# Depthwise taps of the last two tiles, layer norm and second pointwise product taken chunk by chunk, without products on diagonals

## The chip, the core and the metric

The kernel runs on one core of a Trainium2 chip. The metric is the device time of one execution in microseconds (us), the median over several runs. The engines of the core run in parallel: PE (TensorE, matrix products), DVE (VectorE, elementwise), ACT (ScalarE, elementwise with functions and scales), POOL (GpSimd, elementwise) and the queues that issue transfers (SP). Each engine works through its own list of instructions in order, and waits at an instruction until what it needs has been signalled by the others.

## The reference

One step of a two-layer diffusion backbone over 1152 tokens (1024 of a sample, 128 of a prompt) of 1024 features. Layer 0 mixes tokens with a gated depthwise convolution, layer 1 with attention; each is followed by a feed-forward part. Only layer 0's mixer changes here. Cut to what matters:

```python
def conformer_conv(h, w_pw1, dw_w, dw_b, ln_g, ln_b, w_pw2):
    a, g = jnp.split(h @ w_pw1, 2, axis=-1)         # first pointwise product
    u = a * jax.nn.sigmoid(g)                       # gate
    u = dwconv(u, dw_w, dw_b)                       # 31 taps over tokens, each feature by itself
    u = jax.nn.silu(layernorm(u, ln_g, ln_b))       # over the 1024 features of a token
    return u @ w_pw2                                # second pointwise product

def trunk(x, cond, ...):
    for i in range(DEPTH):
        mod = (jax.nn.silu(cond) @ ada_w[i] + ada_b[i])[:, None, :]       # adaLN vectors
        sh1, sc1, g1, sh2, sc2, g2 = jnp.split(mod, N_MOD, axis=-1)
        h = modulate(rmsnorm(x, norm1_g[i]), sh1, sc1)
        ...
            y = conformer_conv(h, ...)
        ...
        x = x + g1 * y
        h = modulate(rmsnorm(x, norm2_g[i]), sh2, sc2)
        x = x + g2 * conv_ffn(h, ffn_w_up[i], ffn_conv_w[i], ffn_conv_b[i], ffn_w_down[i])
```

## The kernel before

**Tiles and chunks.** Features lie on the 128 partitions in 8 tiles j, tokens along the columns in 3 chunks c of 384. A product of 1024 features for one tile and one chunk is 8 steps of the contraction with 3 products each (L247 hi times hi, L248, L249), since operands are split into a high and a low part; one such group has 24 products of 384 columns. Weights come as 512 KB tiles, are split by ACT (`w_hi`, L220) and DVE (`w_lo`, L221).

**The convolution.** For each tile j and chunk c, `gated` makes two such groups (`ppa`, `ppg`), then a sigmoid on ACT (`sg`) and the gate on DVE into `u` (a tile's tokens with the padding between sample and prompt: 1167 columns). The 31 taps of a tile are shared out: DVE takes the first ones with one pass each into PSUM (`da`, L660), ACT scales the last ones into one of two buffers (`tmp`, L650) and POOL adds them into `pacc` (two buffers, L651). A join on DVE adds `da` and `pacc` into `U[c]` (printed as `u`, L666). Tiles 0 to 6 have 12 taps on POOL and 19 on DVE, each pass over all 1167 columns.

**Tile 7** is different: 16 of its taps are products with diagonal matrices (`diag`, L699, `dl`, L706), 3 chunks of 16 products; 8 taps go to POOL and 7 to DVE, chunk by chunk (384, 384 and 399 columns).

**Layer norm** of a chunk (`layer_norm`): mean over features as 8 products with a constant matrix (`mu`, L722, L726), subtraction on DVE (L731), squares on ACT (L738; two buffers, of the same tag `tmp` as the taps), sums on DVE and POOL (L741, L744), the sum over partitions and `rstd` (L325 to L334), its spread over partitions (L342), the multiplication on DVE (L753), silu on ACT (L757), and the split in `ln_h` (ACT, L760) and `ln_l` (DVE, L762). It is a generator: one step of it is put into the program at each `tick()`, so that norms of several chunks run beside taps and products.

**Second pointwise product** (`project_residual`): for each chunk 8 groups of 24 products (`pw2p`), each followed by the residual on DVE into `x1` and by a square (ACT, tag `tmp` again) that POOL adds to `acc1`. After it comes the feed-forward part of layer 0 (`f0pg`, `f0pv`).

**adaLN vectors.** Five further groups of vectors (`ada`) are each 8 steps of 4 products with 512 columns (L270), fed by two transfers of 512 KB a step into three buffers (`adaw`), then a copy (`adar`, ACT), 4 transposes and additions on DVE. Before, their steps come out of the same queue of generators at each `tick()`.

**What sets the order.** The program's instructions are handed to a scheduler that simulates the engines and fixes each engine's list of instructions; work in `tc.high_priority()` is preferred where several are ready. Transfers issued by SP keep the program's order.

Of the kernel before, what the change touches and what calls it, by code (L numbers as in the profile page):

```python
# [32 lines left out]
POOL_TAPS = 12  # L33
# [7 lines left out]
POOL_TAPS_6 = 12  # L41
POOL_TAPS_7 = 8
PE_TAPS = 16
# [36 lines left out]
def tile_hybrid_step(ctx: ExitStack, tc: tile.TileContext, a: dict, outs: list):  # L80
# [17 lines left out]
    def phase(**slots):  # L98
        """SBUF of a phase: so many tiles of so many columns for each tag."""
# [26 lines left out]
    class Banks:  # L126
        """PSUM, cut anew for some phases."""
# [18 lines left out]
    # work that runs beside the products, a step after each of them  # L146
# [24 lines left out]
    # ---- weights, in the order of their use: loads run up to three tiles ahead, the split into hi + lo (both exact  # L171
    # in float32r) one or two ----
# [26 lines left out]
    class Weights:  # L199
# [24 lines left out]
        def ahead(self, splits, loads):  # L224
            """Has everything up to so many tiles from the next one split or loaded."""
# [93 lines left out]
    def token_rstd(pool, parts, name, bank=None):  # L319
        """Sums over features of all parts[f, token], then (mean + eps) ** -0.5, tokens on partitions."""  # L320
# [16 lines left out]
    def spread(pool, v, name, bank=None):  # L337
        """v[token, t] to every partition, tokens along the columns."""
# [183 lines left out]
    def load_x(c):  # L522
        """A chunk's tokens, on partitions, where the low parts of the normed chunks go later."""
# [54 lines left out]
    # conformer: gated pointwise, depthwise over tokens, layernorm, silu, pointwise  # L578
    us = []

    def gated(j, c):
        """The products of a chunk; yields before their gating."""
# [6 lines left out]
        tick()  # L589
        psg = project(pool, wg, H[c], f"ppg{j}_{c}")  # L590
        yield
        tick()
        sg = ntile(f"sg{j}_{c}")
        nc.scalar.activation(sg, psg[:, 0:CH], AF.Sigmoid)
        for lo, hi, cond in pieces(c):
            o = HALF + c * CH + lo + HALF * cond
            nc.vector.tensor_tensor(u[:, o : o + hi - lo], psa[:, lo:hi], sg[:, lo:hi], ALU.mult)
        tick()
        if c == 1:
            weights.ahead(SPLITS, SPLITS)  # L600
# [41 lines left out]
    def taps_pool(j, u, pacc, t0, s0_, s1_):  # L642
        """The taps from t0 on, with the bias."""
# [9 lines left out]
    def taps_vector(j, u, d, n, s0_, s1_, fresh):  # L653
        """The first n taps."""
# [15 lines left out]
    last = KT - 1  # L670
    for j in range(last + 1):
# [6 lines left out]
        if j == 1:  # L678
            bg.append(chain(*(ada(pool, l, g) for l, g in ((0, 1), (0, 2), (1, 0), (1, 1), (1, 2)))))
        if j == last:  # L680
            break
# [3 lines left out]
        t0 = TAPS - (POOL_TAPS if j < last - 1 else POOL_TAPS_6)  # L685
# [6 lines left out]
    # the last tile: some taps as products with diagonals, the others on top of them, chunk by chunk, so that the norm  # L692
    # of a chunk runs beside the taps of the next
    u = us[last][2]
    t0 = TAPS - POOL_TAPS_7
    te = t0 - PE_TAPS
    diag = hp.tile([P, PE_TAPS, P], F32, tag="hh", name="diag")
    for i in range(PE_TAPS):
        nc.scalar.activation(diag[:, i, :], ident, AF.Copy, scale=tap(last, te + i))  # L699
    dl = []  # L700
    for c in range(NCH):
        s0_, s1_ = SPAN[c]
        dl.append(pool("mm", f"dl{c}")[:, 0 : s1_ - s0_])
        for i in range(PE_TAPS):
            t = te + i
            nc.tensor.matmul(  # L706
                dl[c], diag[:, i, :], u[:, s0_ + t : s1_ + t], start=(i == 0), stop=(i == PE_TAPS - 1)
            )

    L = [None] * NCH  # L710
    half = KT // 2
    mus = []
    for c in range(NCH):
        if c == 0:
            mu = pool("mm", "mu0")
        else:
            if c == 1:
                mu_all = pool("acc", "mu").rearrange("p (c n) -> p c n", c=NCH)
            mu = mu_all[:, c]
        mus.append(mu[:, 0:CH])  # L720
        for j in range(last):
            nc.tensor.matmul(mus[c], mean_w, U[c][:, j, :], start=(j == 0), stop=False)  # L722

    def layer_norm(c):
        mu = mus[c]
        nc.tensor.matmul(mu, mean_w, U[c][:, KT - 1, :], start=False, stop=True)  # L726
        hh, hl = htiles(f"ln{c}")
        ss = [None, None]
        for g in range(2):
# [15 lines left out]
            yield  # L745
        yield
        bank = pool("mm", f"lnv{c}")
        rs = token_rstd(pool, ss, f"lnv{c}", bank)
        yield
        pb = spread(pool, rs, f"lnv{c}", bank)  # L750
        for g in range(2):
# [9 lines left out]
            yield  # L761
            nc.vector.tensor_tensor(hl[:, jj, :], U[c][:, jj, :], raw32(hh)[:, jj, :], ALU.subtract)  # L762
        L[c] = (hh, hl)

    pacc = slot("pacc", f"pacc{last}")
    for c in range(NCH):
        taps_pool(last, u, pacc, t0, *SPAN[c])
    for c in range(NCH):
        for _ in taps_vector(last, u, dl[c], te, *SPAN[c], False):
            tick()  # L770
        join(last, dl[c], pacc, c, SPAN[c][0])
        bg.append(layer_norm(c))
        if c == 0:
            tick()
# [12 lines left out]
    for c in range(NCH):  # L787
        while L[c] is None:
            tick()
# [486 lines left out]
```

## Time and profile before

| | |
|---|---|
| median of 3 runs | 2790.17 us (2788.33 to 2790.51) |
| span of the profiled execution (first to last instruction) | 2789.3 us |
| PE busy | 2724.6 us, 98% of the span |
| DVE busy | 1585.4 us, 57% |
| ACT busy | 1053.5 us, 38% |
| POOL busy | 699.6 us, 25% |
| mean granted TensorE clock | 0.991 |

The profiled execution is one of its own, and its time is its span with the little that lies around it; the median stands 0.87 us above the span. A busy share is an average over the whole kernel: the layer-0 mixer, in which the change lies, takes the first 524 us of the 2789.3, and what it costs or gives has to be read there.

### The profile page before, as it was taken

The numbers are of one execution on the slowest core, as the hardware profiler recorded it, in microseconds if no ns is written. First come the engines' busy times: TensorE is split into PE (matmuls) and PEld (weight loads), VectorE is DVE, ScalarE is ACT, GpSimd is POOL, SyncE is SP. The second block draws the span as 40 slices with busy tenths as digits, with TensorE's granted clock in tenths as the row PEclk, the third lists the DMA queues.
The fourth block names the chain that finished last, engine by engine and source line by source line (L and its number), as shares of the span: only waits on it lengthen the run. The fifth ranks groups of instructions, "written<-read, shape, count | busy, mean of one in ns | idle before, by whom it ended". The sixth has DMA issues, their size and how long they took to land.

```text
span 2789.3 us, 40007 instructions
## 1 busy us (share of the span) xinstructions
PE 2724.6 (98%) x15959; PEld 2577.1 (92%) x15959; DVE 1585.4 (57%) x2743; ACT 1053.5 (38%) x2066; POOL 699.6 (25%) x782
## 2 busy tenths in 40 slices
PE   7999989999999999999999899999999999999999
PEld 4867649999999999999999799899999999999998
DVE  6878886544444444445643788766544444444445
ACT  5545546422222221222555777755422122221222
POOL 2777744300000000000555566535000000000003
PEclk9999989999999999999999999999999999999999
DMA  7465425311111111111210000044111111111111
GB/s 261 158 185 160 154 91 176 110 32 46 46 46 46 39 46 38 46 38 46 95 58 1 1 1 1 32 129 136 45 40 46 38 46 39 46 39 45 32 53 69
DMA packets 194419, 192.18 MB, mean 69 GB/s; under 512 B 7072, under 2 KB 173323, under 8 KB 192698
## 3 DMA queue, kind: packets, MB, share of 16 engines
q1 hardware_dynamic: 193946, 189.53, 21.7%
q8 instruction: 126, 2.06, 0.3%
q14 instruction: 59, 0.48, 0.1%
q0 software_dynamic: 288, 0.11, 0.0%
HBM read 175.19 MB, written 14.42 MB: 68 GB/s over the span
## 4 chain that ended last, share of the span: by engine, by line
PE 94%; DVE 3%; DMA 1%; ACT 1%; issue 0%; POOL 0%; SPq 0%; DVEq 0%; ACTq 0%; POOLq 0%
PE f1pd L249 3%; PE f1pd L247 3%; PE f1pd L248 3%; PE f1pg L249 3%; PE f0pg L249 3%; PE f1pg L248 3%; PE f0pg L248 3%; PE f0pv L247 3%; PE f0pg L247 3%; PE f1pv L249 3%; PE f1pg L247 3%; PE f0pv L248 3%; PE f1pv L248 3%; PE f1pv L247 3%; PE f0pv L249 3%; PE f0pd L248 3%
## 5 line engine op out<-in xcount | busy, mean ns | idle before, releaser
L220 ACT ACTIVATE w_hi<-w_raw 128x1024 fp32r<-128x1024 f32 x208 | 218.1, 1058 | 939.4 <-PE f0pd L248 223.7
L221 DVE TENSOR_TENSOR w_lo<-w_raw,w_hi 128x1024 fp32r<-128x1024 f32 x208 | 269.4, 1304 | 425.0 <-ACT w_hi L220 422.4
L651 POOL TENSOR_TENSOR pacc<-pacc,tmp 128x1167 f32<-128x1167 f32 (+2 forms) x98 | 234.2, 2393 | 64.8 <-ACT tmp L650 41.6
L384 DVE SCALAR_TENSOR_TENSOR x<-f1pd,mods,x 128x256 f32<-128x256 f32 (+1 forms) x352 | 170.2, 514 | 102.6 <-PE f1pd L249 102.4
L384 DVE SCALAR_TENSOR_TENSOR x<-f0pd,mods,x 128x256 f32<-128x256 f32 (+1 forms) x352 | 169.8, 514 | 99.1 <-PE f0pd L249 98.9
L660 DVE SCALAR_TENSOR_TENSOR da<-u,dww,da 128x1167 f32<-128x1167 f32 x126 | 180.8, 1435 | 2.8
L1084 POOL TENSOR_TENSOR pr<-pr,sm 128x384 f32<-128x384 f32 x192 | 153.8, 829 | 107.3 <-DVE sm L1082 49.4
L411 POOL MEMSET f1gp<- 128x1 f32 x66 | 3.7, 98 | 703.7 <-DVE f1gp L435 690.5
L411 POOL MEMSET f0gp<- 128x1 f32 x66 | 3.6, 98 | 703.8 <-DVE f0gp L435 690.7
L248 PE MATMUL f1pd<-f1al,w_hi 128*128 128x384 f32 x528 | 178.8, 339 | 0.0
L249 PE MATMUL f1pd<-f1ah,w_lo 128*128 128x384 f32 x528 | 178.7, 338 | 0.0
L249 PE MATMUL f0pd<-f0ah,w_lo 128*128 128x384 f32 x528 | 178.7, 338 | 0.0
L248 PE MATMUL f0pd<-f0al,w_hi 128*128 128x384 f32 x528 | 178.5, 338 | 0.0
L247 PE MATMUL f1pd<-f1ah,w_hi 128*128 128x384 f32 x528 | 178.5, 339 | 0.0
L247 PE MATMUL f0pd<-f0ah,w_hi 128*128 128x384 f32 x528 | 178.0, 338 | 0.0
L249 PE MATMUL f0pg<-n_h,w_lo 128*128 128x384 f32 x528 | 176.7, 335 | 0.0
L249 PE MATMUL f1pg<-n_h,w_lo 128*128 128x384 f32 x528 | 176.7, 335 | 0.0
L248 PE MATMUL f1pg<-n_l,w_hi 128*128 128x384 f32 x528 | 176.7, 335 | 0.0
L248 PE MATMUL f0pv<-n_l,w_hi 128*128 128x384 f32 x528 | 176.7, 335 | 0.0
L248 PE MATMUL f0pg<-n_l,w_hi 128*128 128x384 f32 x528 | 176.7, 335 | 0.0
L247 PE MATMUL f0pg<-n_h,w_hi 128*128 128x384 f32 x528 | 176.7, 335 | 0.0
L247 PE MATMUL f1pg<-n_h,w_hi 128*128 128x384 f32 x528 | 176.7, 335 | 0.0
(327 smaller groups left out, 7802.7 us busy)
## 6 DMA issues: line engine op xcount, KB each, us to landing
adaw<-in_ada_w_dram SPq DMA_DIRECT2D x96, 512.0 KB, 4.4
w_raw<-in_ffn_w_up_dram SPq DMA_DIRECT2D x88, 512.0 KB, 3.8
w_raw<-in_ffn_w_down_dram SPq DMA_DIRECT2D x44, 512.0 KB, 3.9
w_raw<-in_conv_w_pw_dram SPq DMA_DIRECT2D x40, 512.0 KB, 6.8
w_raw<-in_attn_w_o_dram SPq DMA_DIRECT2D x24, 512.0 KB, 4.4
xs_d<-x SPq DMA_DIRECT2D x6, 1536.0 KB, 11.1
x<-xs_d SPq DMA_DIRECT2D x6, 1536.0 KB, 7.8
w_raw<-in_attn_w_qkv_dram SPq DMA_DIRECT2D x12, 512.0 KB, 3.6
```

The source lines that it names most:

```text
L220: nc.scalar.activation(hi, raw, AF.Copy)
L221: nc.vector.tensor_tensor(lo, raw, raw32(hi), ALU.subtract)
L247: nc.tensor.matmul(ps, wh, mh, start=first, stop=False)
L248: nc.tensor.matmul(ps, wh, ml, start=False, stop=False)
L249: nc.tensor.matmul(ps, wl, mh, start=False, stop=last)
L384: nc.vector.scalar_tensor_tensor(xx, ps[:, lo:hi], mod(l, v, j, cond), xx, ALU.mult, ALU.add)
L411: nc.gpsimd.memset(gp[:, z : z + 1], 0.0)
L651: nc.gpsimd.tensor_tensor(d, d, tmp, ALU.add)
L660: nc.vector.scalar_tensor_tensor(d, src, tap(j, t), d, ALU.mult, ALU.add)
L1084: nc.gpsimd.tensor_tensor(pr[n], pr[n], ri.to_broadcast([P, CH]), ALU.mult)
```

## The change

Parts of the diff, without comments and docstrings that go:

```diff
-POOL_TAPS = 12
+POOL_TAPS = 13
...
-POOL_TAPS_6 = 12
-POOL_TAPS_7 = 8
-PE_TAPS = 16
+POOL_TAPS_LATE = 15
+WHOLE = 6
+LATER = (8, 0, 6)
...
     us = []
+    later = chain(*(ada(pool, l, g) for l, g in ((0, 1), (0, 2), (1, 0), (1, 1), (1, 2))))
...
         psa = project(pool, wa, H[c], f"ppa{j}_{c}")
-        tick()
         psg = project(pool, wg, H[c], f"ppg{j}_{c}")
         yield
-        tick()
-        sg = ntile(f"sg{j}_{c}")
...
-        tick()
+        if j:
+            next(later, None)
+        with tc.high_priority():
+            sg = ntile(f"sg{j}_{c}")
...
         if c == 1:
+            if j:
+                next(later, None)
             weights.ahead(SPLITS, SPLITS)
...
-    for j in range(last + 1):
+    for j in range(KT):
...
-        if j == last:
-            break
+        if j >= WHOLE:
+            continue
...
-            nc.tensor.matmul(
-                dl[c], diag[:, i, :], u[:, s0_ + t : s1_ + t], start=(i == 0), stop=(i == PE_TAPS - 1)
-            )
...
+    late = pool("acc", "late").rearrange("p (b n) -> p b n", n=512)
+    paccs = {j: slot("pacc", f"pacc{j}") for j in range(WHOLE, KT)}
+
+    def late_taps(c):
+        s0_, s1_ = SPAN[c]
+        t0 = TAPS - POOL_TAPS_LATE
+        for j in range(WHOLE, KT):
+            u, d = us[j][2], late[:, j - WHOLE, 0 : s1_ - s0_]
+            taps_pool(j, u, paccs[j], t0, s0_, s1_)
+            for _ in taps_vector(j, u, d, t0, s0_, s1_, True):
+                pass
+            join(j, d, paccs[j], c, s0_)
 
     def layer_norm(c):
-        mu = mus[c]
-        nc.tensor.matmul(mu, mean_w, U[c][:, KT - 1, :], start=False, stop=True)
+        mu = late[:, KT - WHOLE, 0:CH]
+        for j in range(KT):
+            nc.tensor.matmul(mu, mean_w, U[c][:, j, :], start=(j == 0), stop=(j == KT - 1))
...
             ps = project(pool, w, H[c], f"{name}p{c}_{m}")
-            residual(ps, X, m, c, l, 2)
-            add_stat(acc, m, c, X[c][:, m, :], tag=tag)
+            with tc.high_priority():
+                residual(ps, X, m, c, l, 2)
+                add_stat(acc, m, c, X[c][:, m, :], tag=tag)
             tick()
+            if l == 0 and m % 2:
+                next(later, None)
...
     for c in range(NCH):
-        while L[c] is None:
-            tick()
+        for _ in range(LATER[c]):
+            next(later, None)
+        late_taps(c)
+        with tc.high_priority():
+            layer_norm(c)
         X[c] = reload(0, c, "x1_")
         project_residual(L, X, c, acc1, 0, "pw2", "tmp")
```

In words: tiles 0 to 5 have 13 taps on POOL and 18 on DVE; tile 7 has no diagonal products any more; tiles 6 and 7 are tapped chunk by chunk, 15 taps on POOL (one starts `pacc` on ACT, 14 are added) and 16 on DVE for each, so 28 additions on POOL for each chunk. The taps of a chunk stand in the program right ahead of its norm and of its second product, and the norm is no generator any more. The steps of the adaLN groups come one with each gating (two with that of the middle chunk), 8 ahead of chunk 0's late taps, 6 ahead of chunk 2's, and one with every second group of the second product.

What the scheduler makes of it at the place where the second product of chunk 0 ends. Rows read: line, operation, output and inputs, shape. On POOL, before: the squares of chunk 0 are added to `acc1`, then comes the norm statistic of the feed-forward part's input (`n10`), and the squares of chunk 1.

```order
L317 TENSOR_TENSOR acc1_3129<-acc1_3129,sq5_0_3378 128x384
L317 TENSOR_TENSOR acc1_3129<-acc1_3129,sq6_0_3420 128x384
L317 TENSOR_TENSOR acc1_3129<-acc1_3129,sq7_0_3456 128x384
L334 TENSOR_TENSOR n10_r_3500<-n10_m_3498,mhalf_93 128x3
L317 TENSOR_TENSOR acc1_3129<-acc1_3129,sq1_1_3534 128x384
L317 TENSOR_TENSOR acc1_3129<-acc1_3129,sq2_1_3573 128x384
```

On POOL, after, at the same place: behind the last square of chunk 0 stand the 28 additions of chunk 1's late taps, of which these are the first four.

```order
L317 TENSOR_TENSOR acc1_2639<-acc1_2639,sq6_0_3138 128x384
L317 TENSOR_TENSOR acc1_2639<-acc1_2639,sq7_0_3173 128x384
L654 TENSOR_TENSOR pacc6_2637<-pacc6_2637,tmp6_17_384_3179 128x384
L654 TENSOR_TENSOR pacc6_2637<-pacc6_2637,tmp6_18_384_3182 128x384
L654 TENSOR_TENSOR pacc6_2637<-pacc6_2637,tmp6_19_384_3185 128x384
L654 TENSOR_TENSOR pacc6_2637<-pacc6_2637,tmp6_20_384_3188 128x384
```

What moved: the taps that chunk 1's norm needs stand behind the end of chunk 0's second product, where before no tap was left. On ACT, before, the square of that last residual (`sq7_0`) is followed by weight splits and by the squares of chunk 1.

```order
L316 ACTIVATE sq6_0_3420<-x1_0_3130 128x384
L760 ACTIVATE ln2_h_3166<-u_2_823 128x1536
L220 ACTIVATE w26_hi_3502<-w26_raw_3428 128x1024
L316 ACTIVATE sq7_0_3456<-x1_0_3130 128x384
L220 ACTIVATE w27_hi_3541<-w27_raw_3465 128x1024
L313 ACTIVATE acc1_3129<-x1_1_3459 128x384
L220 ACTIVATE w28_hi_3614<-w28_raw_3506 128x1024
```

On ACT, after, the same square is followed by the 28 scaled taps of chunk 1 (here the first four); the squares of its norm, `lnsq1`, come behind them.

```order
L316 ACTIVATE sq6_0_3138<-x1_0_2876 128x384
L220 ACTIVATE w26_hi_3397<-w26_raw_3145 128x1024
L316 ACTIVATE sq7_0_3173<-x1_0_2876 128x384
L653 ACTIVATE tmp6_17_384_3179<-u6_2226,dww_139 128x384
L653 ACTIVATE tmp6_18_384_3182<-u6_2226,dww_139 128x384
L653 ACTIVATE tmp6_19_384_3185<-u6_2226,dww_139 128x384
L653 ACTIVATE tmp6_20_384_3188<-u6_2226,dww_139 128x384
```

What moved: `sq7_0` and the scaled taps share the two `tmp` buffers, and the taps stand behind it. On PE, before, the last group of chunk 0's second product (`pw2p0_7`) is followed at once by the first of chunk 1 (`pw2p1_0`).

```order
L249 MATMUL pw2p0_7_3430<-ln0_h_3015,w23_lo_3389 128x384
L247 MATMUL pw2p0_7_3430<-ln0_h_3015,w23_hi_3388 128x384
L248 MATMUL pw2p0_7_3430<-ln0_l_3016,w23_hi_3388 128x384
L249 MATMUL pw2p0_7_3430<-ln0_h_3015,w23_lo_3389 128x384
L247 MATMUL pw2p1_0_3467<-ln1_h_3073,w24_hi_3424 128x384
L248 MATMUL pw2p1_0_3467<-ln1_l_3074,w24_hi_3424 128x384
```

On PE, after, between the two stand the mean of chunk 1 (8 products, into `late`), the sum of its squares (`lnv1`, 128x1) and the spread of its `rstd` (128x128).

```order
L249 MATMUL pw2p0_7_3147<-ln0_h_2828,w23_lo_3107 128x384
L325 MATMUL n10_s_3389<-ones_91,acc1_2639 128x1 x3
L712 MATMUL late_2636<-u_1_822,mean_w_135 128x384 x8
L325 MATMUL lnv1_3326<-ones_91,lnss1_0_3311 128x1
L325 MATMUL lnv1_3326<-ones_91,lnss1_1_3320 128x1
L325 MATMUL lnv1_3326<-ones_91,lnss1_0_3311 128x1
L325 MATMUL lnv1_3326<-ones_91,lnss1_1_3320 128x1
L325 MATMUL lnv1_3326<-ones_91,lnss1_0_3311 128x1
L325 MATMUL lnv1_3326<-ones_91,lnss1_1_3320 128x1
L342 MATMUL lnv1_3326<-ident_86,lnv1_r_3335 128x128 x3
L342 MATMUL n10_b_3432<-ident_86,n10_r_3395 128x128 x3
L247 MATMUL pw2p1_0_3362<-ln1_h_3306,w24_hi_3141 128x384
```

What moved: the mean, the statistics and so the whole norm of chunk 1 lie between the second products of chunks 0 and 1, and the same holds between chunks 1 and 2. From the first product of the feed-forward part on, PE's, POOL's and SP's lists are the same in both kernels.

## Rows read from the trace of the kernel before

**Rows 1.** The page: the span, the chain that ended last by engine, and a costly group.

```profile
span 2789.3 us, 40007 instructions
...
PE 94%; DVE 3%; DMA 1%; ACT 1%; issue 0%; POOL 0%; SPq 0%; DVEq 0%; ACTq 0%; POOLq 0%
...
L221 DVE TENSOR_TENSOR w_lo<-w_raw,w_hi 128x1024 fp32r<-128x1024 f32 x208 | 269.4, 1304 | 425.0 <-ACT w_hi L220 422.4
```

**Rows 2.** Windows: stretch; busy PE, PEld, DVE, ACT, POOL (count); granted clock, DMA share, GB/s.

```profile
80.70:333.40 252.70, 249.27 (x1284) 185.42 (x1283) 207.56 (x189) 127.34 (x134) 200.13 (x88) 0.99 0.56 175
333.40:417.00 83.60, 72.44 (x253) 35.51 (x251) 70.15 (x84) 41.04 (x56) 43.28 (x34) 0.91 0.31 95
417.00:523.70 106.70, 106.68 (x615) 106.68 (x616) 73.13 (x87) 61.38 (x90) 44.22 (x34) 0.97 0.56 169
```

**Rows 3.** Timeline of PE: start, duration, instruction, and the idle time before it.

```profile
80.71 0.44 PE L247 MATMUL ppa<-n_h,w_hi 128*128 128x384 f32 x1
...
333.42 1.78 PE L706 MATMUL dl<-u,diag 128*128 128x384 f32 x5
...
417.02 0.69 PE L248 MATMUL pw2p<-ln_l,w_hi 128*128 128x384 f32 x1 [1.37 <-DVE ln_l L762]
...
422.31 0.40 PE L249 MATMUL pw2p<-ln_h,w_lo 128*128 128x384 f32 x1
...
520.25 0.34 PE L248 MATMUL pw2p<-ln_l,w_hi 128*128 128x384 f32 x1
...
523.72 0.33 PE L247 MATMUL f0pg<-n_h,w_hi 128*128 128x384 f32 x1
```

**Rows 4.** Timeline of PE around one stretch of adaLN products.

```profile
200.11 0.34 PE L249 MATMUL ppa<-n_h,w_lo 128*128 128x384 f32 x1
200.37 1.05 PE L270 MATMUL ada<-adaw,cs 128*32 128x512 f32 x4
201.36 0.45 PE L247 MATMUL ppg<-n_h,w_hi 128*128 128x384 f32 x1
201.64 0.34 PE L248 MATMUL ppg<-n_l,w_hi 128*128 128x384 f32 x1
```

**Rows 5.** Groups by shape, 80 to 420 us: count | busy us, mean ns | idle before.

```profile
L651 POOL TENSOR_TENSOR pacc<-pacc,tmp 128x1167 f32<-128x1167 f32 x77 | 211.7, 2752 | 58.8 <-ACT tmp L650 36.9 <-DMA xs_d<-x 12.0 <-DVE w_lo L221 6.0
L660 DVE SCALAR_TENSOR_TENSOR da<-u,dww,da 128x1167 f32<-128x1167 f32 x126 | 180.8, 1435 | 2.8
...
L221 DVE TENSOR_TENSOR w_lo<-w_raw,w_hi 128x1024 fp32r<-128x1024 f32 x16 | 27.9, 1744 | 21.9 <-ACT w_hi L220 19.4 <-PE ppg L249 1.4 <-PE ppa L249 1.0
```

**Rows 6.** The same view, the shapes of one chunk: taps and layer norm.

```profile
L651 POOL TENSOR_TENSOR pacc<-pacc,tmp 128x384 f32<-128x384 f32 x14 | 14.0, 1003 | 0.9
...
L731 DVE TENSOR_TENSOR u<-u,mu 128x1536 f32<-128x1536 f32 x6 | 10.2, 1750 | 5.4 <-PE mu L726 5.4
...
L650 ACT ACTIVATE tmp<-u,dww 128x384 f32<-128x384 f32 x14 | 8.6, 616 | 8.9 <-POOL pacc L651 8.9
L651 POOL TENSOR_TENSOR pacc<-pacc,tmp 128x399 f32<-128x399 f32 x7 | 8.6, 1231 | 5.1 <-ACT tmp L650 4.7
L660 DVE SCALAR_TENSOR_TENSOR dl<-u,dww,dl 128x384 f32<-128x384 f32 x14 | 8.6, 614 | 3.7 <-PE dl L706 3.7
L738 ACT ACTIVATE lnsq<-u 128x768 f32<-128x768 f32 x10 | 8.2, 840 | 22.4 <-DVE u L731 17.7 <-DVE lnss L741 1.8 <-DVE lnss L744 1.7
...
L744 POOL TENSOR_TENSOR lnss<-lnss,lnsq 128x384 f32<-128x384 f32 x4 | 4.3, 1082 | 2.6 <-ACT lnsq L738 2.4
```

**Rows 7.** Timeline of POOL: additions of taps back to back, 3 of 1167 columns, 14 of 384.

```profile
339.47 23.06 POOL L651 TENSOR_TENSOR pacc<-pacc,tmp 128x1167 f32<-128x1167 f32 x17 [1.40 <-ACT tmp L650]
```

**Rows 8.** Timelines of PE and of ACT in the layer norm.

```profile
405.87 2.29 PE L325 MATMUL lnv<-ones,lnss 128*128 128x1 f32 x10 [0.28 <-POOL lnss L744]
...
410.19 1.65 PE L342 MATMUL lnv<-ident,lnv_r 128*128 128x128 f32 x6 [2.02 <-POOL lnv_r L334]
...
408.00 4.89 ACT L757 ACTIVATE u<-u,vecs 128x384 f32<-128x384 f32 x8
```

More of the change, by code (lines that the diff above doesn't have):

```diff
@@ L588, in gated @@
         psa = project(pool, wa, H[c], f"ppa{j}_{c}")
-        tick()
         psg = project(pool, wg, H[c], f"ppg{j}_{c}")
         yield
-        tick()
-        sg = ntile(f"sg{j}_{c}")
[L594 to L597, printed above, removed]
-        tick()
+        if j:
+            next(later, None)
+        with tc.high_priority():
+            sg = ntile(f"sg{j}_{c}")
+            nc.scalar.activation(sg, psg[:, 0:CH], AF.Sigmoid)
+            for lo, hi, cond in pieces(c):
+                o = HALF + c * CH + lo + HALF * cond
+                nc.vector.tensor_tensor(u[:, o : o + hi - lo], psa[:, lo:hi], sg[:, lo:hi], ALU.mult)
         if c == 1:
+            if j:
+                next(later, None)
             weights.ahead(SPLITS, SPLITS)
@@ L668, in join @@
             )
-    last = KT - 1
-    for j in range(last + 1):
+    for j in range(KT):
         if j:
@@ L677, in tile_hybrid_step @@
                     pass
-        if j == 1:
-            bg.append(chain(*(ada(pool, l, g) for l, g in ((0, 1), (0, 2), (1, 0), (1, 1), (1, 2)))))
-        if j == last:
-            break
+        if j >= WHOLE:
+            continue
         u = us[j][2]
@@ L684, in tile_hybrid_step @@
         pacc = slot("pacc", f"pacc{j}")
-        t0 = TAPS - (POOL_TAPS if j < last - 1 else POOL_TAPS_6)
+        t0 = TAPS - POOL_TAPS
         taps_pool(j, u, pacc, t0, 0, CONV_N)
@@ L690, in tile_hybrid_step @@
             join(j, da, pacc, c)
[L694 to L705, printed above, removed]
-            nc.tensor.matmul(
-                dl[c], diag[:, i, :], u[:, s0_ + t : s1_ + t], start=(i == 0), stop=(i == PE_TAPS - 1)
-            )
     L = [None] * NCH
     half = KT // 2
[L712 to L722, printed above, removed]
+    late = pool("acc", "late").rearrange("p (b n) -> p b n", n=512)
[9 more added lines that the diff above has]
+            join(j, d, paccs[j], c, s0_)
     def layer_norm(c):
-        mu = mus[c]
-        nc.tensor.matmul(mu, mean_w, U[c][:, KT - 1, :], start=False, stop=True)
+        mu = late[:, KT - WHOLE, 0:CH]
+        for j in range(KT):
+            nc.tensor.matmul(mu, mean_w, U[c][:, j, :], start=(j == 0), stop=(j == KT - 1))
         hh, hl = htiles(f"ln{c}")
@@ L744, in layer_norm @@
                         eng.tensor_tensor(ss[g], ss[g], sq[:, o : o + CH], ALU.add)
-            yield
-        yield
         bank = pool("mm", f"lnv{c}")
         rs = token_rstd(pool, ss, f"lnv{c}", bank)
-        yield
         pb = spread(pool, rs, f"lnv{c}", bank)
@@ L760, in layer_norm @@
             nc.scalar.activation(hh[:, jj, :], U[c][:, jj, :], AF.Copy)
-            yield
             nc.vector.tensor_tensor(hl[:, jj, :], U[c][:, jj, :], raw32(hh)[:, jj, :], ALU.subtract)
         L[c] = (hh, hl)
[L765 to L769, printed above, removed]
-            tick()
[L771 to L774, printed above, removed]
     def project_residual(H, X, c, acc, l, name, tag):
@@ L787, in tile_hybrid_step @@
     for c in range(NCH):
-        while L[c] is None:
-            tick()
+        for _ in range(LATER[c]):
[3 more added lines that the diff above has]
+            layer_norm(c)
         X[c] = reload(0, c, "x1_")
@@ L792, in tile_hybrid_step @@
         bg.append(norm_mod(pool, X, acc1, c, 0, 1, H, "n1"))
+    for _ in later:
+        pass
     pool.open(mm=(5, 512), t=(2, 512), ms=(1, 512))
```

## Prediction

> **What bounds the kernel now.** I read the page first, then the kernel cut into stretches, then single instructions on either side of the change. On the page the chain that ended last lies on PE for 94% of the span [rows 1]: where PE stands idle, the kernel gets longer, and what other engines do beside a busy PE costs nothing. The stretches say where PE is idle [rows 2]. In the first (gated products, whole taps) it is busy 249.27 of 252.70 us, in the third (second pointwise product) 106.68 of 106.70; only the middle one, from the first diagonal product to the second product, has a gap worth the name, 72.44 of 83.60, and a part of that work is the diagonal products themselves. So before, norms and taps are nearly all covered by products. The marks that I measure against are the timeline's [rows 3]: gated products from 80.71, diagonals from 333.42, second product in earnest from 417.02, feed-forward part from 523.72. From that last mark PE's, POOL's and SP's lists are the same in both kernels, so I take the remaining 2265.6 us as unchanged and ask only when that product starts.
>
> **First stretch.** Two things leave PE here. Up to the last gated product the order has 128 products of adaLN before and 88 after: 40 fewer. A record of "x4" covers two such products and takes 200.37 to 201.36, 0.99 us [rows 4]; 20 of those are 19.8 us. They stand in 57 stretches before and in 23 after. A change of stream costs 0.26 us going in and 0.28 coming back, where two products of a steady stream are 0.1735 apart (20 from 520.25 to 523.72 [rows 3]): 0.19 a stretch, 34 fewer, 6.5 us. So the last gated product, which I call P, ends at 333.4 - 19.8 - 6.5 = 307.1, if PE still bounds. POOL now needs 12 additions of 2.752 us a tile, 33 us; DVE 18 taps of 1.435, two splits of 1.744 [rows 5] and some 3.5 of joins and gates, 33 us. Six tiles are 198 us, from about 87 on: both are done with their share by some 286, ahead of P, but in the after order a part of tile 5 stands behind the last sigmoid. This term could be 3.4 us less (the part of 252.70 in which PE was idle, if it goes) or, by the first rival, 17 more.
>
> **From P to the first mean.** Behind P, ACT scales three whole taps of tile 5 and waits once for four pairs of adaLN products (4.0 us); POOL is done with tile 5 about 11.7 us after P (three additions of 2.752 behind it). DVE has 7 taps of 1.435 left, the additions of an adaLN group and the joins, till P + 17.6. The third buffer wanted for `pacc` is free only then, and ACT, which waits for it behind four scaled taps of tile 6, holds POOL up for some 3 us. Then POOL has 28 additions of 384 columns. Alone they take 1.003 us, the 399 ones 1.231 [rows 6]; in a row of 17 without a pause, 23.06 us less three of 2.752 leave 14.80 for 14, 1.06 each [rows 7], which I take: 29.7 us. ACT's 0.616 and DVE's 32 taps of 0.614 (19.7) lie beside it. With the join and the mean behind it the sum is 11.7 + 3 + 29.7 + 1.6, so the mean is there at P + 46 = 353.1.
>
> **A norm by itself.** Now nothing runs beside it on PE. Two subtractions of 1.75; then squares (0.84), sums (two of about 0.61 on DVE, two of 1.08 on POOL [rows 6]) that take turns on two buffers: 3.5 + 0.6 + 1.2 + 0.84 + 2.2, and four hand-overs of 0.28 [rows 8], 9.4 us. From the first sum over partitions to the spread 405.87 to 410.19, 4.3; the spread 1.65; a multiplication 1.75; eight silus 4.89; then the copy and the subtraction of the first half, priced at 1.75 each as passes of that size: **25.5 us** from mean to second product. It could be 2 less if the copy and the hand-overs are cheaper, and 10 more if the 16 taps of the next chunk that DVE has in between (16 x 0.614) all come first.
>
> **The second product of a chunk.** 192 products of 0.1735 are 33.3 us. They start slowly after an idle stretch: before, the 17 steps from 417.02 to 422.31 are 0.311 apart [rows 3], and the granted clock of that stretch is 0.97 in the mean where a steady one has 0.99 [rows 2]; 17 x 0.138 = 2.4 us, now three times. Chunks 0 and 1 also carry 8 products of adaLN (four pairs, 4.3). So 40.0, 40.6 with a group's transposes, and 36.3 for the last.
>
> **Between the chunks.** This is the term that decides. In the order that stands above, POOL has the 28 additions of chunk 1 behind the last square of chunk 0, ACT the scaled taps behind that square, and PE's next product is chunk 1's mean. So while 29.7 us of additions run, PE has nothing to do: residual, square and addition of the last group (2.3), 29.7, join and mean 1.5, together **33.5 us**, and then the 25.5 of the norm. For chunk 2 the taps are 399 columns wide (+1.2), and the copy of an adaLN group stands among ACT's taps and waits for 24 products that are fed by transfers: 0 to 8 us, I take 4. So 38.7. Taps and joins of the next chunk that DVE does already beside the norm do not help, since POOL is the longer of the two.
>
> **The sum.** 307.1 + 46.0 = 353.1; norm 378.6; second product 418.6. Up to here it is as late as before (417.02), though with all of chunk 0 done by then. Then +33.5 = 452.1, +25.5 = 477.6, +40.6 = 518.2, +38.7 = 556.9, +25.5 = 582.4, +36.3 = 618.7. Before, the feed-forward part starts at 523.72: 95.0 us later, a span of 2884.3, and with the 0.87 us by which the median of the runs stands above the profiled span (2790.17 against 2789.3) **2885 us**. The diagonal products are saved, and that gain is inside the sum: the second product starts 38 us earlier (378.6), and more than three times that is given back.
>
> **Rivals.** *Splits held up by POOL.* In the first stretch a split `w_lo` takes 1.744 us in the mean, over the whole kernel, where POOL is mostly quiet, 1.304 [rows 1, 5]. If each of the 14 splits that fall beside POOL's additions waited through a whole one of 2.752, DVE would need 38 us more, 21 of which fit before P: +17, **2902 us**. Against it speaks that the mean is only 0.44 longer. The Trainium skill ("SBUF — State Buffer", section "Who interferes with whom") says that a DVE instruction with two SBUF inputs contends with a GpSimd one that reads SBUF, that whoever comes first holds the shared ports for a whole instruction and the other blocks; by that rule this rival would hold. The trace agrees only in direction: 0.44 us and not up to 2.75. Chance 0.05.
>
> *The next chunk's taps are done beside the second product.* If POOL and ACT came to them earlier than I read, say because the squares wait and the taps do not, the 33.5 and 38.7 us would vanish and the norm alone would show: 2884.3 - 72.2 + 0.9 = **2813 us**. POOL has the time for it (it is busy 44 of 106.7 us in that stretch [rows 2]), its list speaks against it. Chance 0.05.
>
> *Other sign: taps and norm are both covered.* One place, the step from the second product of a chunk to the next. If PE went on there as before, the exposed 59.0 and 64.2 us would go: 2884.3 - 123.2 - 4.8 (two slow starts) + 0.9 = **2757 us**, faster than before by the diagonals and the adaLN stretches. It decides where the two waits together fall by 95 us, to about 14 us each. PE's order, with the mean, the sums and the spread of chunk 1 ahead of its second product, speaks against it. Chance 0.03.
>
> **How the numbers follow.** Forecast 0.85, the rivals 0.05, 0.05 and 0.03, anything beyond 0.02. The forecast's own bounds: POOL's addition from 1.003 to 1.231 us, 84 times (-5 to +14); the adaLN copy -4 to +4; P -3 to +17; three norms -6 to +30. Not all at once: low 2858, high 2925, which holds the first rival and leaves out the others. A change of 0.2% (5.6 us) is about what a measurement of this kernel can tell from none. Faster 0.03, same 0.01, slower 0.96.
>
> **What would show it.** In the profile after: the last `ppg` ending near 307; the first `pw2p` near 379; two gaps of PE of about 59 and 64 us between the groups of `pw2p`, inside which POOL adds 28 times without a pause and ACT's `tmp` waits for POOL; a chain that ended last with some 4% on POOL; `f0pg` starting near 619. I am wrong if POOL's additions of chunk 1 run beside `pw2p` of chunk 0, or if the rest behind `f0pg` does not keep its 2265.6 us.

## The result, and the profile after

The changed kernel takes **2887.84 us** in the median of four executions against 2790.34 us of the kernel before: a ratio of 1.0348 (95% interval 1.0331 to 1.0364), 97 us slower. One of the four took 6854.49 us and is left out of that ratio; the other three lie between 2884.51 and 2887.97. Its profiled execution has a span of 2885.8 us. The page's lines that answer to those of [rows 1]:

```profile
span 2885.8 us, 40019 instructions
...
PE 87%; DVE 6%; POOL 3%; DMA 2%; ACT 2%; issue 1%; SPq 0%; DVEq 0%; POOLq 0%; ACTq 0%
```

PE's share of the chain that ended last has gone from 94% to 87%; DVE, POOL, ACT and transfers have taken its place. Where, the stretches say; I cut them where the timeline has its marks (columns as in [rows 2]):

```profile
80.70:289.30 208.60, 208.60 (x1205) 180.18 (x1207) 196.00 (x169) 117.73 (x114) 192.28 (x82) 1.00 0.53 167
289.30:371.30 82.00, 33.11 (x105) 11.86 (x103) 62.64 (x81) 37.99 (x53) 46.87 (x38) 0.65 0.26 83
371.30:408.50 37.20, 37.16 (x205) 34.70 (x205) 14.63 (x15) 11.24 (x16) 8.87 (x6) 0.95 0.72 212
408.50:474.00 65.50, 15.76 (x51) 11.00 (x50) 36.33 (x53) 29.89 (x47) 34.01 (x34) 0.58 0.00 1
474.00:512.10 38.10, 37.78 (x213) 35.00 (x217) 18.42 (x23) 16.11 (x25) 13.04 (x10) 0.96 0.83 248
512.10:582.70 70.60, 28.72 (x97) 13.03 (x97) 26.93 (x40) 30.46 (x48) 36.19 (x35) 0.67 0.21 67
582.70:619.50 36.80, 35.60 (x193) 34.92 (x194) 20.58 (x33) 16.09 (x24) 14.50 (x10) 0.95 0.60 175
619.50:2885.80 2266.30, 2235.75 (x13482) 2203.79 (x13480) 1185.09 (x2286) 780.28 (x1695) 388.50 (x587) 1.00 0.15 46
```

Read downwards: gated products with PE never idle; tail of the taps and the first norm; then the three second products of 37 to 38 us, with two stretches of 65.5 and 70.6 us between them in which PE is busy for 16 and 29 us only. The last row is the rest of the kernel, 2266.3 us against 2265.6 before. So the whole loss lies ahead of the feed-forward part, which starts at 619.53 and not at 523.72. The timeline of PE at those marks, answering to [rows 3]:

```profile
288.92 0.34 PE L249 MATMUL ppg<-n_h,w_lo 128*128 128x384 f32 x1
...
339.45 7.82 PE L712 MATMUL late<-u,mean_w 128*128 128x384 f32 x16 [17.45 <-DVE u L669]
...
371.34 0.69 PE L248 MATMUL pw2p<-ln_l,w_hi 128*128 128x384 f32 x1 [0.47 <-DVE ln_l L744]
...
411.62 0.61 PE L325 MATMUL n_s<-ones,acc 128*128 128x1 f32 x4 [3.08 <-POOL acc L317]
...
442.03 7.73 PE L712 MATMUL late<-u,mean_w 128*128 128x384 f32 x16 [29.58 <-DVE u L669]
...
473.97 0.69 PE L248 MATMUL pw2p<-ln_l,w_hi 128*128 128x384 f32 x1 [0.47 <-DVE ln_l L744]
...
551.90 7.41 PE L712 MATMUL late<-u,mean_w 128*128 128x384 f32 x16 [15.28 <-DVE u L669]
...
619.53 0.33 PE L247 MATMUL f0pg<-n_h,w_hi 128*128 128x384 f32 x1
```

PE waits 29.58 us at 442.03 for the join of chunk 1's last tapped tile (`u`, L669); the mean takes another 7.7 us, and the second product goes on at 473.97. What the join waited for stands in POOL's timeline:

```profile
278.40 30.68 POOL L654 TENSOR_TENSOR pacc<-pacc,tmp 128x1167 f32<-128x1167 f32 x13
312.55 0.99 POOL L654 TENSOR_TENSOR pacc<-pacc,tmp 128x384 f32<-128x384 f32 x1 [3.48 <-ACT tmp L653]
314.27 24.53 POOL L654 TENSOR_TENSOR pacc<-pacc,tmp 128x384 f32<-128x384 f32 x23 [0.72 <-ACT tmp L653]
...
410.01 1.55 POOL L317 TENSOR_TENSOR acc<-acc,sq 128x384 f32<-128x384 f32 x1 [2.58 <-ACT sq L316]
411.52 29.86 POOL L654 TENSOR_TENSOR pacc<-pacc,tmp 128x384 f32<-128x384 f32 x28
...
515.07 15.43 POOL L654 TENSOR_TENSOR pacc<-pacc,tmp 128x399 f32<-128x399 f32 x14
535.77 15.42 POOL L654 TENSOR_TENSOR pacc<-pacc,tmp 128x399 f32<-128x399 f32 x14 [5.27 <-ACT tmp L653]
```

The 28 additions of chunk 1 begin the moment the last square of chunk 0 is added (410.01 + 1.55) and run for 29.86 us without a pause, 1.07 us each. For chunk 2 they are two runs of 14 with a hole of 5.27 us, in which ACT's list stands at the copy of an adaLN group. (A row names the first shape only: the 13 of the first row are nine whole additions and four of 384 columns.)

### The profile page after: what moved, and what is told of

Its sections match the earlier page's. It is cut to its first block, busy times and chain, and to the rows that moved or that the text cites. A ratio compares the mean times of both kernels' runs of the same rounds, so it can differ in the third digit from the quotient of the medians.

```text
span 2885.8 us, 40019 instructions
## 1 busy us (share of the span) xinstructions
PE 2692.8 (93%) x15863; PEld 2568.6 (89%) x15863; DVE 1608.9 (56%) x2793; ACT 1083.1 (38%) x2110; POOL 758.8 (26%) x840
## 4 chain that ended last, share of the span: by engine, by line
PE 87%; DVE 6%; POOL 3%; DMA 2%; ACT 2%; issue 1%; SPq 0%; DVEq 0%; POOLq 0%; ACTq 0%
PE f1pd L247 3%; PE f1pd L249 3%; PE f1pd L248 3%; PE f1pg L249 3%; PE f0pg L249 3%; PE f1pg L248 3%; PE f0pg L248 3%; PE f0pv L247 3%; PE f1pv L247 3%; PE f0pg L247 3%; PE f1pg L247 3%; PE f1pv L248 3%; PE f0pv L248 3%; PE f0pv L249 3%; PE f1pv L249 3%; PE f0pd L247 3%
## 5 line engine op out<-in xcount | busy, mean ns | idle before, releaser
L221 DVE TENSOR_TENSOR w_lo<-w_raw,w_hi 128x1024 fp32r<-128x1024 f32 x208 | 280.6, 1358 | 425.9 <-ACT w_hi L220 425.7
L654 POOL TENSOR_TENSOR pacc<-pacc,tmp 128x1167 f32<-128x1167 f32 (+2 forms) x156 | 291.4, 1870 | 36.1 <-ACT tmp L653 13.5
L653 ACT ACTIVATE tmp<-u,dww 128x1167 f32<-128x1167 f32 (+2 forms) x156 | 142.6, 918 | 97.0 <-POOL pacc L654 94.6
```

Source lines behind the costliest of these rows:

```text
L221: nc.vector.tensor_tensor(lo, raw, raw32(hi), ALU.subtract)
L653: nc.scalar.activation(tmp, u[:, s0_ + t : s1_ + t], AF.Copy, scale=tap(j, t))
L654: nc.gpsimd.tensor_tensor(d, d, tmp, ALU.add)
```

## The experiments

Three theories were open behind the total. **A**: it is the order; the squares of the second product and the scaled taps share two buffers, so the next chunk's taps cannot begin before the second product ends. **B**: it is the amount; without diagonal products DVE and POOL have more to do than PE can cover, wherever it stands. And for the first stretch, **C**: adaLN products cost PE by stretch and not, as I had it, by product. All ratios are to the kernel before in the same session.

**Run 1, squares in other buffers.**

```diff
-        project_residual(L, X, c, acc1, 0, "pw2", "tmp")
+        project_residual(L, X, c, acc1, 0, "pw2", None)
```

Expected:

> The changed kernel with one edit: the squares of the second product's residuals take their buffers from the general pool of 384-column tiles and not from the two tmp buffers that the scaled taps use. Nothing else moves in the program. Theory (the two shared buffers force the taps of chunk 1 behind the last square of chunk 0, and so put 28 POOL additions and a norm in PE's way): the additions of chunk 1 now run beside the second product of chunk 0, its mean falls among the groups of pw2p0, the two waits of PE between the second products shrink from 65 and 71 us to 15 to 30 us each, span near 2795 (2780 to 2815). Rival (the amount of taps on POOL and DVE without the diagonal products is what costs, wherever they stand): the waits stay within 10 us of what they were, span above 2870.

Measured: 2829.44 us, ratio 1.0143 (1.0126 to 1.0160); span 2826.3. The mean of chunk 1 now lies among the second products of chunk 0, PE:

```profile
399.08 5.38 PE L712 MATMUL late<-u,mean_w 128*128 128x384 f32 x16
...
427.18 2.29 PE L325 MATMUL lnv<-ones,lnss 128*128 128x1 f32 x10 [2.88 <-POOL lnss L730]
...
442.03 0.69 PE L247 MATMUL pw2p<-ln_h,w_hi 128*128 128x384 f32 x1 [7.90 <-ACT ln_h L743]
...
443.82 0.69 PE L248 MATMUL pw2p<-ln_l,w_hi 128*128 128x384 f32 x1 [0.47 <-DVE ln_l L744]
```

One word takes 59.5 us of span off, 61% of the loss, with the same taps on the same engines. A is shown for that part of the loss: the wait between chunks 0 and 1 falls from 65.4 us (408.54 to 473.97) to 26.2 (417.65 to 443.82), that between 1 and 2 from 71 to 27. But I had expected a span near 2795. The norm of chunk 1 now takes 39.4 us from mean to second product where it took 24.2 alone, because splits, residuals and the next taps stand between its passes on DVE and ACT. On DVE, the first sum of its squares comes 12 us behind its subtraction:

```profile
404.49 3.42 DVE L717 TENSOR_TENSOR u<-u,late 128x1536 f32<-128x1536 f32 x2 [2.41 <-PE late L712]
...
418.76 1.22 DVE L221 TENSOR_TENSOR w_lo<-w_raw,w_hi 128x1024 fp32r<-128x1024 f32 x1
419.89 1.35 DVE L727 TENSOR_TENSOR lnss<-lnsq 128x384 f32<-128x384 f32 x1
```

Each mean costs the second product that it is in some 5 us. The hidden norm takes longer, and the second products slow down with it: those of chunks 0 and 1 take 43.4 and 55.1 us where they took 37.2 and 38.1. In the 55.1, PE also stands idle for 8.7, for splits on ACT and DVE and for adaLN transfers.

**Run 2, the norm ahead as well.**

```diff
     for c in range(NCH):
+        if c + 1 < NCH:
+            ...
+            late_taps(c + 1)
+            with tc.high_priority():
+                layer_norm(c + 1)
         X[c] = reload(0, c, "x1_")
-        project_residual(L, X, c, acc1, 0, "pw2", "tmp")
+        project_residual(L, X, c, acc1, 0, "pw2", None)
```

> The first edit, and in the program the late taps and the layer norm of chunk c+1 stand ahead of the second product of chunk c. Theory: the norm (24 us) is covered as well, but the mean of chunk 1 now stands ahead of the first second product on PE, so that this one starts later by part of the 30 us of additions; the two later waits fall to about 10 us each. Feed-forward start near 517, span near 2783 (2765 to 2800). Rival (amount of taps): span above 2850.

Measured: 2820.66 us, ratio 1.0107 (1.0092 to 1.0123). The direction is right, the size is not. The second product of chunk 2 follows that of chunk 1 without a pause (518.46 to 518.63), so there taps and norm are wholly hidden; but PE's list holds the mean of chunk 1 and the first sum of its squares ahead of the very first second product, which starts at 410.4 in place of 371.3 (39 us), and those of chunk 2 ahead of chunk 1's (29 us). Why the scheduler put them there, no run shows. A wait on PE was moved, and only one of the two was removed.

**Run 3, the kernel before with the adaLN steps spread as after.** One part of the change alone:

```diff
         psa = project(pool, wa, H[c], f"ppa{j}_{c}")
-        tick()
         psg = project(pool, wg, H[c], f"ppg{j}_{c}")
         yield
-        tick()
+        if j:
+            next(later, None)
...
-        tick()
         if c == 1:
+            if j:
+                next(later, None)
```

> The kernel before with one part of the change alone: the adaLN steps come one with each gating and one more with the middle chunk, not at three ticks for each chunk, so that ahead of the last gate product there are 88 products in 23 stretches and not 128 in 57; what is left is ticked beside taps and norms as before. Theory (a stretch costs PE about 1.1 us whether it holds two products or four, since the four of a step run side by side): the last gate product ends near 292 in place of 333, DVE and POOL with the whole taps of tile 6 (some 320) bound then, second product starts 15 to 35 us earlier than 417, span 2755 to 2775. Rival (each pair of products costs 0.99 us, as the prediction had it): the last gate product ends near 307, and the end is at the same place, as DVE bounds anyhow.

Measured: 2785.9 us, ratio 0.9992 (0.9982 to 1.0001): no change that can be told. The last gate product ends near 289 as C has it, 44 us earlier, and nearly nothing of it reaches the end (the feed-forward part starts at 518.7, 5 us earlier). PE, then DVE, behind it:

```profile
357.67 1.05 PE L270 MATMUL ada<-adaw,cs 128*32 128x512 f32 x4 [1.62 <-DMA adaw<-in_ada_w_dram]
360.05 1.05 PE L270 MATMUL ada<-adaw,cs 128*32 128x512 f32 x4 [1.33 <-DMA adaw<-in_ada_w_dram]
361.29 1.05 PE L270 MATMUL ada<-adaw,cs 128*32 128x512 f32 x4 [0.19 <-DMA adaw<-in_ada_w_dram]
...
355.29 1.55 DVE L668 TENSOR_TENSOR u<-da,pacc 128x384 f32<-128x384 f32 x4
363.87 3.42 DVE L732 TENSOR_TENSOR u<-u,mu 128x1536 f32<-128x1536 f32 x2 [7.03 <-PE mu L727]
```

DVE has its last whole tap at 355, where it was 378 before, so about half of the 44 us is lost by then; and it waits 7 us more for the mean, because PE's list has adaLN products, each waiting for its transfer, ahead of it. Further ones stand in the first second products.

**Run 4, stretches halved.** In the changed kernel, each step of four adaLN products is cut in two:

```diff
+                if q == 1 and (l or grp):
+                    yield
             yield
```

with twice as many places that take a step.

> The changed kernel with each adaLN step of four products cut into two stretches of two, so that 96 products stand in 41 stretches ahead of the last gate product, in place of 88 in 23. Theory (price by stretch, 1.1 us with its change of stream 0.19): the last gate product ends 18 x 1.3 = 23 us later, near 312. Rival (price by product, 0.5 each, and 0.19 a stretch): 8 x 0.5 + 18 x 0.19 = 7 us later, near 297. In both POOL, done with the whole taps only at 309, covers most of it, so the end moves by under 15 us.

Measured, one execution: 2908.15 us, span 2906.3. The last gate product ends at 307.2, 18 us later than in the changed kernel (289.3): 18 more stretches, 1.0 us each. C is nearer (23) than price by product (7). The rows of the changed kernel show why. These are a stretch of two products and one of four:

```profile
254.01 1.05 PE L270 MATMUL ada<-adaw,cs 128*32 128x512 f32 x4
258.51 1.06 PE L270 MATMUL ada<-adaw,cs 128*32 128x512 f32 x8
```

Two products and four cost the same: each of the four of a step has 32 columns of weights ("128*32") and an output quarter of its own. The Trainium skill ("TensorEngine Tiling (Array Packing)", section "Key Properties") says that such tiles can run in parallel; the two rows agree, 1.05 us against 1.06. My expectation that POOL would cover the delay was wrong: the first mean starts 16 us later (355.66 against 339.45) and the end comes 20 us later, since the taps of a tile wait for its gates (POOL's run of additions that holds tile 5's last ones ends at 320.9 in place of 309.1), and since POOL then stands 6.64 us more while ACT's list is at an adaLN copy.

**Run 5, spread adaLN with the rest placed early**, on run 3:

```diff
-            bg.append(later)
...
+    for _ in range(6):
+        next(later, None)
     L = [None] * NCH
...
             tick()
+            if l == 0 and m % 2:
+                next(later, None)
```

> The third run's kernel (before, adaLN steps one with each gating) with the rest of the adaLN steps placed otherwise: six right behind the diagonal products, where PE is idle until DVE has the last taps, then one with every second group of the second product, none at the ticks of taps and norms. Theory (in the third run the gain of 44 us at the last gate product was eaten because 72 adaLN products, fed by transfers, stood in PE's list among the means of the norms, from 325 to 362, and in two-product stretches in the first second products, 397 to 423): the last product of chunk 0's mean comes near 342 and not 362, second product in earnest near 385, feed-forward part near 497, span 2750 to 2775. Rival (DVE's and POOL's taps bound, which end at 357 whatever PE does): within 8 us of the third run's 2783.5.

Measured: 2794.02 us, ratio 1.0014 (1.0004 to 1.0023). The second product starts in earnest at 390 and the feed-forward part at 505.74, 18 us ahead of before, and yet the kernel is not faster; its span of 2792.1 is outside the theory's range and just above the rival's. The gain is lost behind the mark, on PE:

```profile
521.80 0.80 PE L325 MATMUL n_s<-ones,acc 128*128 128x1 f32 x6 [0.79 <-ACT adar L279]
523.80 0.93 PE L342 MATMUL n_b<-ident,n_r 128*128 128x128 f32 x6 [1.19 <-POOL n_r L334]
526.08 0.46 PE L247 MATMUL f0pg<-n_h,w_hi 128*128 128x384 f32 x1 [1.35 <-ACT n_h L363]
```

The statistic `n_s` of chunk 1 waits for `adar`, the copy that empties the PSUM bank of the last adaLN group: both use the one bank `ms`, and the leftover steps hold it until 521.

**Run 6, the mean in a bank of its own**, in the changed kernel:

```diff
-        mu = late[:, KT - WHOLE, 0:CH]
+        mu = pool("mm", f"mu{c}")[:, 0:CH]
```

> The changed kernel, the mean of a norm in a PSUM bank of its own and not in the tile that the late taps of DVE are summed in. Theory (all 8 products of the mean, 7.8 us, stand behind the last join because they share that tile): six of the eight run before the last join, and each of the three norms starts 5 to 6 us earlier; span 2866 to 2874. Rival (the mean is late for another reason, so the order of its products is worth nothing): 2883 to 2888.

Measured: 2879.07 us, ratio 1.0319 (1.0305 to 1.0333); span 2876.1, 9.7 us less. The means of chunk 0 on PE:

```profile
328.91 1.65 PE L712 MATMUL mu<-u,mean_w 128*128 128x384 f32 x2
339.04 1.65 PE L712 MATMUL mu<-u,mean_w 128*128 128x384 f32 x2 [8.48 <-DVE u L669]
```

Only the last of the eight products is left behind the last join, so the shared tile was what held the other seven. Seven products (6 us) come off the first wait, and off the later ones too, but there the products that now run early stand among the second products (4 us each). So 9.7 and not 12 to 20.

**Run 7, half of POOL's additions left out** for chunks 1 and 2:

```diff
-            nc.gpsimd.tensor_tensor(d, d, tmp, ALU.add)
+            if s0_ == 0 or (t - t0) % 2 == 0:
+                nc.gpsimd.tensor_tensor(d, d, tmp, ALU.add)
```

> The changed kernel with every second of POOL's additions left out for chunks 1 and 2 (so these outputs lack those taps; ACT still scales them, DVE is unchanged). Theory (between the chunks PE waits for POOL's 28 additions one for one until DVE's taps of tile 7, 9.8 us behind the join of tile 6, become the longer path): both waits 12 to 15 us shorter, span 2856 to 2862. Rival (the wait is DVE's or ACT's, POOL only fills it): above 2876.

Measured, one execution: 2868.83 us, span 2867.0, 18.8 us less. DVE behind the second product of chunk 0:

```profile
420.87 0.56 DVE L670 TENSOR_TENSOR u<-late,pacc 128x384 f32<-128x384 f32 x1 [9.34 <-POOL pacc L655]
421.46 0.62 DVE L662 TENSOR_SCALAR late<-u,dww 128x384 f32<-128x384 f32 x1
422.12 9.84 DVE L664 SCALAR_TENSOR_TENSOR late<-u,dww,late 128x384 f32<-128x384 f32 x15
432.06 0.56 DVE L670 TENSOR_TENSOR u<-late,pacc 128x384 f32<-128x384 f32 x1
```

Each wait is some 10 us shorter with 15 us of additions fewer: POOL leads, and DVE's 16 taps of tile 7 behind the join of tile 6 follow close. The span lies between the range (up to 2862) and the rival (from 2876): POOL was the longer path by 10 us a chunk, not more.

**Run 8, runs 1 and 6 together**, with `LATER = (12, 0, 0)`.

> The changed kernel with the squares in the general pool (first run), the mean in its own bank, and the adaLN steps that stood ahead of chunk 2's taps moved ahead of chunk 0's (12 there, where PE is idle). Theory (in the first run the wait ahead of chunk 2's second product was 27 us because adaLN products fed by transfers stood on PE between 481 and 523, and the means cost 5 us each inside the second product): span 2785 to 2812. Rival (what is left is the norm itself, slowed by the splits, squares and taps beside it): 2818 to 2830.

Measured: 2830.09 us, ratio 1.0147 (1.0133 to 1.0161), no better than run 1. The span of 2828.3 is in the rival's range, but not for the rival's reason: the mean of chunk 2 is done at 481.5, its second product starts at 527. In between DVE, ACT and POOL norm the feed-forward part's input of chunks 0 and 1, which had been put off, and chunk 0's statistic waits there for the copy `adar` of an adaLN group (491.99) as in run 5. Taking one wait out of the chain let the next piece of work in.

**Runs 9 and 10, towards a faster kernel**, on run 5. Run 9 gives the last adaLN group a bank that the means leave free and puts 10 steps, not 6, behind the diagonal products; run 10 has 6 steps there and 24 diagonal taps:

```diff
-    later = chain(*(ada(pool, l, g) for l, g in ((0, 1), (0, 2), (1, 0), (1, 1), (1, 2))))
+    later = chain(
+        *(ada(pool, l, g) for l, g in ((0, 1), (0, 2), (1, 0), (1, 1))), ada(lambda tag, name: mu_all[:, 0], 1, 2)
+    )
...
-POOL_TAPS_7 = 8
-PE_TAPS = 16
+POOL_TAPS_7 = 7
+PE_TAPS = 24
```

(the second part in run 10 alone, which also takes five adaLN steps in each second product and not four.)

> The fifth run's kernel with two edits: the last adaLN group sums in a PSUM bank that the means leave free, not in the one bank that the statistics of the feed-forward part's input need too, and ten adaLN steps, not six, stand behind the diagonal products. Theory (in the fifth run the feed-forward part started at 505.7 but stood still soon after, since the statistic of chunk 1 had to wait until 521.8 for that bank): the start stays near 505 and nothing stands still behind it, span 2766 to 2778. Rival (what holds the feed-forward part up is the norm work on DVE): 2786 to 2794.

> As the ninth run with 24 taps of tile 7 as diagonal products in place of 16 (7 taps on POOL and ACT, none on DVE), and five adaLN steps in each second product. Theory (DVE's taps, which end at 357, set the first norm; 21 taps of 0.62 us fewer bring them to 344, and PE has idle time for 16 us more of products): second product some 10 us earlier than in the ninth run, span 2756 to 2770. Rival (POOL, which ends at 347, or PE with its products and the adaLN steps is the next bound): 2770 to 2780.

Measured: 2781.41 us, ratio 0.9975 (0.9965 to 0.9985), and 2777.41 us, ratio 0.9957 (0.9944 to 0.9969). Both beat the kernel before, by 0.25% and 0.43%, and both miss their range: run 9's span of 2778.7 is just above it, run 10's 2773.8 is in its rival's. In run 9 the feed-forward part starts at 515.9 and nothing stands still behind it. For the bank as the cause in run 5 it speaks that chunk 1's statistic now runs at 481.23, ahead of the last steps of that group (485 to 506); but four steps fewer are left over as well, and no run separates the two. The ten steps keep PE until 364, so the norm starts later again. In run 10 DVE has its last join at 346.4 in place of 356.1 in run 9 and goes straight into the norm:

```profile
344.85 1.54 DVE L670 TENSOR_TENSOR u<-da,pacc 128x384 f32<-128x384 f32 x4
346.31 0.24 DVE L287 TENSOR_TENSOR mods<-adat,adab 128x16 f32<-128x16 f32 x2
...
347.05 3.42 DVE L735 TENSOR_TENSOR u<-u,mu 128x1536 f32<-128x1536 f32 x2 [0.29 <-PE mu L730]
```

More diagonal products bring DVE to the norm sooner while PE has room. That they shorten the kernel is not shown by this alone: run 10 moves adaLN steps too, and the ratios of the two runs differ by less than their intervals.

**Run 11, no diagonal products**, in the kernel before: another part of the change alone.

```diff
-POOL_TAPS_7 = 8
-PE_TAPS = 16
+POOL_TAPS_7 = 13
+PE_TAPS = 0
```

> The kernel before with one other part of the change alone: no taps of tile 7 as diagonal products, 18 on DVE and 13 on POOL and ACT, chunk by chunk; norms, adaLN and second product as before. Theory (DVE and POOL set when the norms start, PE has room): 33 more taps of 0.62 us on DVE, 15 more additions of 1.06 on POOL, second product 12 to 20 us later, span 2800 to 2812. Rival (the diagonal products stood in PE's way, 32 us of them): 2765 to 2789.

Measured: 2799.24 us, ratio 1.0037 (1.0024 to 1.0051); the feed-forward part starts 6.7 us later. The span of 2796.0 lies between the theory's range (from 2800) and the rival's (up to 2789). B is true in sign, and worth about 10 us of the 97: with the norms still pipelined, moving 16 taps from PE to DVE and POOL costs this much.

## Why the prediction was right, and which of its terms were not

The forecast was 2885 us, measured 2887.84; the feed-forward part was to start at 618.7 and did at 619.5. The deciding term was the right one, but that the total came so near is luck: errors of 18 and 12 us and more cancel. Step by step, forecast and measured (ends of PE's timeline):

| step | forecast us | measured us | reached, forecast | reached, measured |
|---|---|---|---|---|
| last gated product | | | 307.1 | 289.3 |
| from there to the mean of chunk 0 | 46.0 | 58.0 | 353.1 | 347.3 |
| norm | 25.5 | 24.1 | 378.6 | 371.3 |
| second product, chunk 0 | 40.0 | 37.2 | 418.6 | 408.5 |
| wait and mean of chunk 1 | 33.5 | 41.2 | 452.1 | 449.8 |
| norm | 25.5 | 24.2 | 477.6 | 474.0 |
| second product, chunk 1 | 40.6 | 38.1 | 518.2 | 512.1 |
| wait and mean of chunk 2 | 38.7 | 47.2 | 556.9 | 559.3 |
| norm | 25.5 | 23.5 | 582.4 | 582.8 |
| second product, chunk 2 | 36.3 | 36.7 | 618.7 | 619.5 |

- **The first stretch was mis-sized by 18 us.** I priced 40 adaLN products at half of a two-product record each. They cost by stretch: 34 fewer at 1.08 us (1.25 from the product ahead of one to the product behind it, less 0.17 [rows 4]) and the idle time gone, 3.4, make 40 of the 44.1 us (252.70 - 208.60); the rest has no source here. Run 4 bears this out with 1.0 us a stretch. The trace of before has a stretch of four products too, 1.06 us at 275.35; it would have shown this ahead.
- **From there to the mean was mis-sized by 12 us the other way.** With PE earlier, POOL and DVE are what is late, and DVE more so. POOL has tile 5's whole additions done at 304.8, 15.6 us behind the last gated product where I had 11.7, and four of tile 6 at 309.1; DVE's joins end at 311.2, 21.9 behind it where I had 17.6. As I had it, ACT waits for those joins with the next `pacc`, and POOL stands 3.48 us at 312.55 (POOL, DVE, ACT):

```profile
304.84 4.23 POOL L654 TENSOR_TENSOR pacc<-pacc,tmp 128x384 f32<-128x384 f32 x4
...
309.61 1.55 DVE L669 TENSOR_TENSOR u<-da,pacc 128x384 f32<-128x384 f32 x4
...
311.20 0.71 ACT L648 ACTIVATE pacc<-u,vecs,dww 128x384 f32<-128x384 f32 x1 [3.63 <-DVE u L669]
```

  And the mean took 7.8 us and not a part of 1.6, all eight products standing behind the last join. I had taken the first seven to be done ahead; run 6 shows that they can be, once the mean has its own bank.
- **The deciding step was right.** Additions of 1.07 us, 28 in a row, begin where chunk 0's second product ends, then the norm; run 1 shows that the shared buffers make it so, run 7 that POOL leads by some 10 us, with DVE next. The two waits were each 8 us longer than forecast: 7 of it is the mean again.
- **The norm, 25.5 forecast and 24 measured,** and the second products, 3 us too long each for chunks 0 and 1 (two stretches of adaLN and not four pairs), were close.
- **Rivals.** That the splits are held up by POOL came true as a mechanism, not as a bound. Up to 309 us the changed kernel has

```profile
L221 DVE TENSOR_TENSOR w_lo<-w_raw,w_hi 128x1024 fp32r<-128x1024 f32 x16 | 42.2, 2638 | 7.6 <-ACT w_hi L220 7.6
```

  2.638 us for a split that took 1.744 before [rows 5]. Single ones take from 1.22 us to 3.71, so the longest lost 2.5, nearly a whole POOL addition (2.752). The rule of the Trainium skill that the prediction names ("SBUF — State Buffer", "Who interferes with whom") agrees with such waits. I had argued against it from the mean before, "0.44 us and not up to 2.75"; but single splits of before take up to 3.71 us too, and the mean hid them (DVE, before):

```profile
108.06 3.71 DVE L221 TENSOR_TENSOR w_lo<-w_raw,w_hi 128x1024 fp32r<-128x1024 f32 x1
```

  The longer splits cost DVE 14.3 us. DVE was done with tile 5 some 5 us later than POOL, so what it cost the end can be estimated from POOL's two pauses behind it, 3.48 and 0.72 us: at most some 4 us, and not 17. That the taps hide beside the second product, I gave 0.05; run 1 is that kernel, and it gives 2829, not the 2813 I had worked out. Its two waits, 26.2 and 26.8 us, are close to the bare norm of 25.5 in that sum; what the sum lacks is the 43.4 and 55.1 us of its first two second products, where it has 40.0 and 40.6.

What stays open: how much of the 97 us is the missing overlap of the norms apart from that of the taps. Run 1 gives back 59.5 us of span by the taps; run 2, which was to give back the norms too, moved a wait to the front instead.

## What to carry to other kernels

When two kinds of work draw on one ring of buffers, the ring can set their order, as the two `tmp` buffers did here for 59.5 us: look for the first instruction of the later work right behind the last of the earlier one on two engines at once. Where work is put beside other work, price it at its duration in company (a norm 24 us alone, 39.4 beside a second product), and ask which bank or buffer it takes from the next stage. And a term that comes out of a mean over records should be checked against single records, and records of another length, in the same trace: both the stretch of four and the long splits stood in the one of before.

## What the runs showed of the hardware that I had not expected

Two adaLN products of 32 weight columns took PE 1.05 us and four 1.06. A DVE split with two SBUF inputs beside POOL's additions took 2.638 us in the mean and up to 3.71, 1.261 in the mean of the later stretches (309 to 600 us) of the same execution. And the granted clock falls to 0.58 in the mean of the stretch in which PE waits for chunk 1, so mostly to the lower of its two levels (1.2 of 2.4 GHz). The mean of a norm took 7.73 us there (at a granted clock of 0.70) and 5.38 among second products in run 1 (at 1.00). Behind the wait the second product starts slowly, as [rows 3] show of before, and runs its stretch of 38 us at 0.96.
